# Batch normalisation of 64 tiles: from one DMA ring in phases of two to two DMA rings, with another placement of channels and parameters

## The chip, the cores and the metric

The kernel runs on one core of a Trainium2 chip. Its time is the device time of one execution in microseconds (us); where several runs are given, the median. One further execution was recorded by the hardware profiler, and all views below are of that one. The engines that matter here are SyncE (SP), which issues DMAs and does no arithmetic; VectorE (DVE); ScalarE (ACT), which computes and can issue DMAs too; GpSimd (POOL), which issues DMAs that its software describes; and the 16 DMA engines, which move the data between the main memory (HBM) and the on-chip memory (SBUF, 128 partitions).

## The reference

```python
# x: [32, 256, 128, 128] float32; the four parameters: [256] float32
def reference(x, gamma, beta, running_mean, running_var):
    eps = 1e-5
    mean = running_mean.reshape(1, -1, 1, 1)
    var = running_var.reshape(1, -1, 1, 1)
    gamma = gamma.reshape(1, -1, 1, 1)
    beta = beta.reshape(1, -1, 1, 1)
    return gamma * (x - mean) / np.sqrt(var + eps) + beta
```

Each of the 256 channels has one scale, gamma / sqrt(var + eps), and one shift, beta - mean x scale. Every element is read once, multiplied and added once, and written once: 536.87 MB in and as much out.

## The kernel before

The input is cut into 64 tiles, one for each image and each half of its channels. A tile has 128 channels on 128 partitions and 16384 floats (64 KB) in each: 8.39 MB. Channel p of the half lies on partition p (lines 38 and 39). Three buffers hold tiles (NBUF, line 11), 64 KB a partition each.

All big DMAs, loads (line 48) and stores (line 97), are issued by SP, so they lie in one ring and run in the order of issue. At first three loads are issued. Then the loop at line 100 goes through the tiles in pairs (K = 2): VectorE transforms two tiles in place (line 86, one instruction a tile), SP issues the two stores, and then two loads, of the tiles three further on, each into the buffer of a tile just stored. The framework sets the waits: a store waits for VectorE, a load for the store that frees its buffer. The ring so sees two stores, two loads, two stores, and so on.

The parameters come at the start. GpSimd issues four DMAs (line 56), each of which spreads 256 values over 128 partitions, two to a partition, element by element. ScalarE takes the square root (line 71) and VectorE works out scale and shift in lines 78 to 81. The first tile's transform needs both.

Of the kernel before, what the change touches and what calls it, by code (L numbers as in the profile page):

```python
# [1 line left out]

# [4 lines left out]


SINGLE_QUEUE = True  # L10
NBUF = 3


@with_exitstack
def kernel(
    ctx: ExitStack,
    tc: tile.TileContext,
    x: bass.AP,
    gamma: bass.AP,
    beta: bass.AP,  # L20
    running_mean: bass.AP,
    running_var: bass.AP,
    out: bass.AP,
):
    nc = tc.nc
    eps = 1e-5

    N, C, H, W = x.shape
    P = nc.NUM_PARTITIONS
    assert C % P == 0  # L30
    NCB = C // P
    HW = H * W
    NT = N * NCB

    params = ctx.enter_context(tc.tile_pool(name="params", bufs=1))
    data = ctx.enter_context(tc.tile_pool(name="data", bufs=NBUF))

    xr = x.rearrange("n (cb p) h w -> (n cb) p (h w)", p=P)
    outr = out.rearrange("n (cb p) h w -> (n cb) p (h w)", p=P)

    tiles = {}
    loads = {}

    def issue_load(i):
        if i >= NT:
            return
        t = data.tile([P, HW], mybir.dt.float32, tag="t")
        loads[i] = nc.sync.dma_start(out=t[:], in_=xr[i])  # L48
        tiles[i] = t

    for i in range(NBUF):
        issue_load(i)

    def load_param(ap_1d):
        t = params.tile([P, NCB], mybir.dt.float32, tag=ap_1d.tensor.name)
        nc.gpsimd.dma_start(out=t, in_=ap_1d.rearrange("(j p) -> p j", p=P))  # L56
        return t

    var_t = load_param(running_var)
    gamma_t = load_param(gamma)  # L60
    beta_t = load_param(beta)
    mean_t = load_param(running_mean)

    eps_t = params.tile([P, 1], mybir.dt.float32, tag="eps")
    nc.vector.memset(eps_t, eps)  # L65

    scale_t = params.tile([P, NCB], mybir.dt.float32, tag="scale")
    shift_t = params.tile([P, NCB], mybir.dt.float32, tag="shift")
    tmp_t = params.tile([P, NCB], mybir.dt.float32, tag="tmp")

    nc.scalar.activation(  # L71
        out=tmp_t[:],
        in_=var_t[:],
        func=mybir.ActivationFunctionType.Sqrt,
        bias=eps_t[:],
        scale=1.0,
    )
    nc.vector.reciprocal(out=tmp_t[:], in_=tmp_t[:])  # L78
    nc.vector.tensor_mul(out=scale_t[:], in0=gamma_t[:], in1=tmp_t[:])  # L79
    nc.vector.tensor_mul(out=tmp_t[:], in0=mean_t[:], in1=scale_t[:])  # L80
    nc.vector.tensor_sub(out=shift_t[:], in0=beta_t[:], in1=tmp_t[:])  # L81

    def compute(i):
        t = tiles[i]
        cb = i % NCB
        nc.vector.tensor_scalar(  # L86
            out=t[:],
            in0=t[:],
            scalar1=scale_t[:, cb : cb + 1],
            scalar2=shift_t[:, cb : cb + 1],  # L90
            op0=mybir.AluOpType.mult,
            op1=mybir.AluOpType.add,
        )

    def store(i):
        t = tiles.pop(i)
        (nc.sync if SINGLE_QUEUE else nc.scalar).dma_start(out=outr[i], in_=t[:])  # L97

    K = NBUF - 1
    for b in range((NT + K - 1) // K):  # L100
        idxs = [i for i in range(K * b, K * b + K) if i < NT]
        for i in idxs:
            compute(i)
        for i in idxs:
            store(i)
        for i in idxs:
            issue_load(i + NBUF)


# [1 line left out]
_INS = ['x', 'gamma', 'beta', 'running_mean', 'running_var']  # L111
_OUTS = [((32, 256, 128, 128), 'float32')]


# [23 lines left out]
```

## Time and profile before

| what | value |
|---|---|
| median of 8 runs | 2487.67 us (2486.35 to 2489.26) |
| the profiled execution's own time | 2486.76 us |
| its span, first to last instruction | 2484.7 us |
| moved by DMA, and mean rate over the span | 1073.77 MB, 432 GB/s |
| one VectorE transform of a tile | 8.81 us, 64 of them |
| load, median from issue to landing | 38.6 us |
| store, median from issue to landing | 49.8 us |
| parameter DMAs, issue to landing | 10.8, 15.4, 19.7 and 21.7 us |
| first transform starts | 25.72 us |

The page gives busy times for each engine; a DMA's time from issue to landing includes its place in the ring behind earlier ones. In the timeline a line has start, duration, engine, line of the kernel and operation; "SPq" is SP's queue, where merged issues ("x2") have the time from the first issue to the end of the last, waits between them included. What stands in brackets is the engine's idle time before, and what ended it. In the table of windows, each line has the stretch, its length, the busy time of VectorE, ScalarE and GpSimd with the number of instructions, TensorE's clock, the busy share of the 16 DMA engines, and the rate in GB/s.

### The profile page before, as it was taken

The numbers are of one execution on the slowest core, as the hardware profiler recorded it, in microseconds if no ns is written. First come the engines' busy times: TensorE is split into PE (matmuls) and PEld (weight loads), VectorE is DVE, ScalarE is ACT, GpSimd is POOL, SyncE is SP. The second block draws the span as 40 slices with busy tenths as digits, with TensorE's granted clock in tenths as the row PEclk, the third lists the DMA queues.
The fourth block names the chain that finished last, engine by engine and source line by source line (L and its number), as shares of the span: only waits on it lengthen the run. The fifth ranks groups of instructions, "written<-read, shape, count | busy, mean of one in ns | idle before, by whom it ended". The sixth has DMA issues, their size and how long they took to land.

```text
span 2484.7 us, 378 instructions
## 1 busy us (share of the span) xinstructions
DVE 564.7 (23%) x69; ACT 1.6 (0%) x2; POOL 3.2 (0%) x8
## 2 busy tenths in 40 slices
DVE  2122211222112221122211222122221212212121
ACT  0000000000000000000000000000000000000000
POOL 0000000000000000000000000000000000000000
DMA  9999999999999999999999999999999999999999
GB/s 405 439 436 425 437 434 428 438 434 435 430 435 436 427 436 437 433 431 439 433 429 438 437 433 430 438 432 435 435 434 436 430 438 432 436 434 434 436 430 397
DMA packets 18562, 1073.77 MB, mean 432 GB/s; under 512 B 2176, under 2 KB 2176, under 8 KB 2176
## 3 DMA queue, kind: packets, MB, share of 16 engines
q1 hardware_dynamic: 18432, 1073.75, 99.9%
q0 software_dynamic: 128, 0.00, 0.0%
q14 instruction: 2, 0.02, 0.0%
HBM read 536.88 MB, written 536.87 MB: 432 GB/s over the span
## 4 chain that ended last, share of the span: by engine, by line
DMA 51%; another core or an unknown queue 36%; DVE 11%; SPq 0%; issue 0%; POOL 0%; DVEq 0%; POOLq 0%; PEldq 0%
DMA t<-in_x_dram 48%; DVE t L86 11%; DMA out_dram<-t 2%; DMA t<-in_running_mean_dram 1%; SPq L97 0%; POOL t L56 0%; DVEq L86 0%; POOLq L133 0%; SPq L48 0%; DVE tmp_t L80 0%; DVE shift_t L81 0%; DVEq L80 0%; PEldq L133 0%
## 5 line engine op out<-in xcount | busy, mean ns | idle before, releaser
L86 DVE TENSOR_SCALAR t<-t,scale_t,shift_t 128x16384 f32<-128x16384 f32 x64 | 564.0, 8812 | 1864.4 <-DMA t<-in_x_dram 1864.4
L78 DVE RECIPROCAL tmp_t<-tmp_t 128x2 f32<-128x2 f32 x1 | 0.2, 165 | 12.9 <-ACT tmp_t L71 12.9
L80 DVE TENSOR_TENSOR tmp_t<-t,scale_t 128x2 f32<-128x2 f32 x1 | 0.2, 160 | 7.6 <-DMA t<-in_running_mean_dram 7.6
L71 ACT ACT_TABLE_LOAD x1 | 1.3, 1283 | 12.1 <-DMA t<-in_running_var_dram 12.1
L79 DVE TENSOR_TENSOR scale_t<-t,tmp_t 128x2 f32<-128x2 f32 x1 | 0.2, 161 | 3.7 <-DMA t<-in_gamma_dram 3.7
L56 POOL DMA_DIRECT2D t<-in_running_var_dram x1 | 0.8, 837 | 0.8 <-PEq L133 0.8
L56 POOL DMA_DIRECT2D t<-in_gamma_dram x1 | 0.7, 722 | 0.0
L56 POOL DMA_DIRECT2D t<-in_beta_dram x1 | 0.7, 720 | 0.0
L56 POOL DMA_DIRECT2D t<-in_running_mean_dram x1 | 0.7, 720 | 0.0
L71 ACT ACTIVATE tmp_t<-t,eps_t 128x2 f32<-128x2 f32 x1 | 0.3, 295 | 0.0
L65 DVE MEMSET eps_t<- 128x1 f32 x1 | 0.1, 59 | 0.8 <-PEq L122 0.8
L81 DVE TENSOR_TENSOR shift_t<-t,tmp_t 128x2 f32<-128x2 f32 x1 | 0.2, 160 | 0.0
L122 POOL MEMSET const-bfloat16-1.0<- 128x1 bf16 x1 | 0.1, 95 | 0.0
L122 POOL MEMSET const-float32-0.0<- 128x1 f32 x1 | 0.1, 93 | 0.2 <-issue 0.2
L122 POOL MEMSET const-uint8-127<- 128x1 uint8 x1 | 0.1, 93 | 0.0
L122 POOL MEMSET const-float32-1.0<- 128x1 f32 x1 | 0.1, 92 | 0.0
## 6 DMA issues: line engine op xcount, KB each, us to landing
t<-in_x_dram SPq DMA_DIRECT2D x64, 38.6
out_dram<-t SPq DMA_DIRECT2D x64, 49.8
t<-in_running_var_dram POOLq DMA_DIRECT2D x1, 1.0 KB, 10.8
t<-in_gamma_dram POOLq DMA_DIRECT2D x1, 1.0 KB, 15.4
t<-in_beta_dram POOLq DMA_DIRECT2D x1, 1.0 KB, 19.7
t<-in_running_mean_dram POOLq DMA_DIRECT2D x1, 1.0 KB, 21.7
```

The costliest lines, as they stand in the source:

```text
L56: nc.gpsimd.dma_start(out=t, in_=ap_1d.rearrange("(j p) -> p j", p=P))
L65: nc.vector.memset(eps_t, eps)
L71: nc.scalar.activation(out=tmp_t[:], in_=var_t[:], func=mybir.ActivationFunctionType.Sqrt, bias=eps_t[:], scale=1.0,)
L78: nc.vector.reciprocal(out=tmp_t[:], in_=tmp_t[:])
L79: nc.vector.tensor_mul(out=scale_t[:], in0=gamma_t[:], in1=tmp_t[:])
L80: nc.vector.tensor_mul(out=tmp_t[:], in0=mean_t[:], in1=scale_t[:])
L81: nc.vector.tensor_sub(out=shift_t[:], in0=beta_t[:], in1=tmp_t[:])
L86: nc.vector.tensor_scalar(out=t[:], in0=t[:], scalar1=scale_t[:, cb : cb + 1], scalar2=shift_t[:, cb : cb + 1], op0=mybir.AluOpType.mult, ...
L122: nc = _bacc.Bacc("TRN2", target_bir_lowering=False, num_devices=1)
```

## The change

- The kernel no longer leaves its waits to the framework: it has a semaphore for each buffer's loads and stores, one for VectorE's finished parts and a few for the start, and each instruction's wait is written out.
- Loads stay on SP; stores go to ACT's queue, each waiting for its tile's transform. There are no pairs any more: tile i's load waits for the store of tile i - 3, the transform for the load, the store for the transform.
- Channels are placed otherwise: channel 16k + e of a half lies on partition 8e + k, in loads and stores alike. The DRAM side of a DMA so has the form 16 x 8 x 16384.
- The parameters come as rows: SP loads each vector of 256 values as one row of 1 KB, copied to 16 partitions, between the left and the right half of load 0. VectorE puts each row into the order of the partitions, transposes it in 32 x 32 blocks, and copies four pieces of the result to the partitions' columns. Square root, scale and shift are worked out as before.
- Tile 0 is loaded and transformed in two halves. Of the last tile, VectorE transforms the first 9216 columns and ScalarE the other 7168.

```diff
-    xr = x.rearrange("n (cb p) h w -> (n cb) p (h w)", p=P)
-    outr = out.rearrange("n (cb p) h w -> (n cb) p (h w)", p=P)
+    xr = x.rearrange("n (cb k e) h w -> (n cb) e k (h w)", k=NK, e=NE)
+    outr = out.rearrange("n (cb k e) h w -> (n cb) e k (h w)", k=NK, e=NE)
...
-        t = params.tile([P, NCB], mybir.dt.float32, tag=ap_1d.tensor.name)
-        nc.gpsimd.dma_start(out=t, in_=ap_1d.rearrange("(j p) -> p j", p=P))
...
+        nc.sync.dma_start(out=bufs[0][:, left], in_=xr[0][:, :, left]).then_inc(early, 16)
+        zeroed = step(nc.vector.memset(rows[:], 0.0))
+        for r, ap in enumerate((running_var, gamma, beta, running_mean)):
+            inst = nc.sync.dma_start(out=rows[0:NE, r * C : (r + 1) * C], in_=ap.partition_broadcast(NE))
+            if r == 0:
+                inst._wait_ge(vec, zeroed)
+            inst.then_inc(fetched, 16)
+        nc.sync.dma_start(out=bufs[0][:, right], in_=xr[0][:, :, right]).then_inc(loaded[0], 16)
+        for i in range(1, NT):
+            s, turn = i % NBUF, i // NBUF
+            inst = nc.sync.dma_start(out=bufs[s][:], in_=xr[i]).then_inc(loaded[s], 16)
+            if turn:
+                inst._wait_ge(stored[s], 16 * turn)
...
+        step(
+            nc.vector.tensor_copy(
+                out=lined.rearrange("p (rc e k) -> p rc e k", e=NE, k=NK),
+                in_=rows.rearrange("p (rc k e) -> p rc e k", k=NK, e=NE),
+            ),
+            fetched,
+            16 * NPAR,
         )
...
+        step(nc.vector.transpose(out=turned[:], in_=lined[:]))
...
+        for q in range(NQ):
+            placed = step(nc.vector.tensor_copy(out=flat[q * B : (q + 1) * B], in_=blocks[:, :, q, 0]))
...
-        (nc.sync if SINGLE_QUEUE else nc.scalar).dma_start(out=outr[i], in_=t[:])
...
+            nc.scalar.dma_start(out=outr[i], in_=bufs[s][:])._wait_ge(done, after).then_inc(stored[s], 16)
...
-    K = NBUF - 1
-    for b in range((NT + K - 1) // K):
-        idxs = [i for i in range(K * b, K * b + K) if i < NT]
-        for i in idxs:
-            compute(i)
-        for i in idxs:
-            store(i)
-        for i in idxs:
-            issue_load(i + NBUF)
...
+        compute(0, left)._wait_ge(early, 16)
+        compute(0, right)._wait_ge(loaded[0], 16)
+        store(0, 2)
+        for i in range(1, last):
+            compute(i)._wait_ge(loaded[i % NBUF], 16 * (i // NBUF + 1))
+            store(i, i + 2)
...
+        compute(last, slice(0, VCOLS))._wait_ge(loaded[last % NBUF], 16 * turns)
+        t, cb = bufs[last % NBUF], last % NCB
+        nc.scalar.activation(
+            out=t[:, VCOLS:],
+            in_=t[:, VCOLS:],
+            func=mybir.ActivationFunctionType.Identity,
+            bias=shift_t[:, cb : cb + 1],
+            scale=scale_t[:, cb : cb + 1],
+        )._wait_ge(loaded[last % NBUF], 16 * turns).then_inc(done, 1)
+        store(last, last + 3)
```

## The prediction

> **What bounds the kernel now.** I read the page's busy times and DMA row first, then the queues, then the waits, then the timeline for the cadence, then windows of the DMA rate for the two ends.
>
> ```profile
> DVE 564.7 (23%) x69; ACT 1.6 (0%) x2; POOL 3.2 (0%) x8
> DMA  9999999999999999999999999999999999999999
> q1 hardware_dynamic: 18432, 1073.75, 99.9%
> q0 software_dynamic: 128, 0.00, 0.0%
> L86 DVE TENSOR_SCALAR t<-t,scale_t,shift_t 128x16384 f32<-128x16384 f32 x64 | 564.0, 8812 | 1864.4 <-DMA t<-in_x_dram 1864.4
> ```
>
> VectorE works a quarter of the span and waits for loads for the rest of it. The one hardware queue fills 99.9% of what 16 DMA engines have. So the kernel is 1073.75 MB pushed through a full pipe, and only two things can move it: the rate of the pipe, and the time in which part of it is empty.
>
> ```profile
> 83.10 19.92 SPq L48 DMA_DIRECT2D t<-in_x_dram  x2
> 103.07 28.08 SPq L97 DMA_DIRECT2D out_dram<-t  x2
> 121.96 8.81 DVE L86 TENSOR_SCALAR t<-t,scale_t,shift_t 128x16384 f32<-128x16384 f32 x1 [49.35 <-DMA t<-in_x_dram]
> 141.78 8.81 DVE L86 TENSOR_SCALAR t<-t,scale_t,shift_t 128x16384 f32<-128x16384 f32 x1 [11.01 <-DMA t<-in_x_dram]
> 161.10 19.70 SPq L48 DMA_DIRECT2D t<-in_x_dram  x2
> ...
> 2406.59 0.34 SPq L48 DMA_DIRECT2D t<-in_x_dram  x1
> 2407.03 47.45 SPq L97 DMA_DIRECT2D out_dram<-t  x2
> ```
>
> This is the cadence: a pair of loads is issued as a pair of stores lands, 78.0 us after the last pair (161.10 - 83.10). Such a period moves four tiles of 8.39 MB. The timeline has the same issue at 1092.57, so 13 early periods take (1092.57 - 83.10) / 13 = 77.65 us, and the 17 later ones (2406.59 - 1092.57) / 17 = 77.30 us, or 19.32 us for a tile and 434 GB/s. The late cadence is the pipe's own; the early periods are 13 x 0.35 = 4.6 us longer.
>
> ```profile
> 0.00:5.00 5.00, 0.06 (x1) 0.00 (x0) 3.19 (x8) 1.00 0.76 262
> 5.00:10.00 5.00, 0.00 (x0) 0.00 (x0) 0.00 (x0) 1.00 1.02 367
> 10.00:25.00 15.00, 0.33 (x2) 1.58 (x2) 0.00 (x0) 1.00 1.01 420
> 1213.00:1985.00 772.00, 175.26 (x21) 0.00 (x0) 0.00 (x0) 1.00 1.00 434
> 2448.00:2484.70 36.70, 6.11 (x1) 0.00 (x0) 0.00 (x0) 1.00 0.85 368
> ```
>
> The last two columns are DMA share and GB/s. The start runs below 434, and in the last 37 us the mean engine is busy only 85% of the time: 5.5 us each. The engines don't finish together, and the slowest ends the kernel.
>
> **The budget of the profiled span.** 128 tile transfers x 19.32 = 2473.5 us. The third load lands at 63.79 (its VectorE instruction starts then), where three tiles would take 58.0: start 5.8 us. Early periods: 4.6. After the last cadence point, 2406.59 + 4 x 19.32 = 2483.9: end 0.8. Sum 2484.7, the span. No more than about 11 us can be won while the rate stays: 0.45%.
>
> [...]
> **The change, part by part.**
> *Parameters.* Removed: four POOL DMAs of 4-byte elements (the 128 packets of q0), which land 10.8 to 21.7 us after issue. Added: four SP DMAs of 1 KB rows in 16 copies[...], queued between the two halves of load 0. The first load took 24.3 us to land (the least of the issue-to-landing times)[...]. A 1 KB row at a 16th of 434 GB/s is 0.04 us; with overhead I take 0.1, four for each engine 0.4, and as much for the split load's second completion. So between 0 and 3.0 us are won, and I take 3.0 - 0.8 = 2.2. SP waits for a memset of 32x1024 before the parameter DMAs[...]. Behind it wait the right half of load 0 and loads 1 and 2; the left half already queued covers 9.7 us, so nothing is lost[...].
> *Turning by VectorE.* A copy and a transpose of 32x1024, four small copies, the square root with its table load (1.28 + 0.29 in the trace), and four operations of 0.16 each. [...]Cost 0: loads 1 and 2 keep the pipe full to about 60 us, and the first store merely comes near 30 instead of 34.56. It would have to be 30 us late to be felt.
> *Two rings.* Stores move from SP behind the load issues to ACT behind VectorE's semaphore; loads on SP wait for their buffer's store only. With both rings always filled, each gets half the rate: load 38.6, VectorE 8.8, store 38.6[...]: 90 us for a buffer's round, and three buffers at 38.6 a tile give it 116. So 26 us of slack: the pipe does not run dry, and no new wait is exposed. Cost of alternation itself, not seen in the trace: between 0 and 1% of rate[...]; I take 0.
> *Dealt channels.* [...]By number of packets and bytes nothing changes. Whether the 4.6 us of the early periods and the 5.5 us of uneven ends are address collisions is unknown: between 0 and 9 us won[...], or a loss if the same pattern collides elsewhere. I take 4.2, a little less than half.
> *Shared last tile.* VectorE does 9216 of 16384 columns, 4.96 us by proportion of 8.81, ScalarE the rest. In the half-rate picture, when load 63 lands the store of tile 62 has some 13 us to go, so even 8.8 us was hidden: 0, and at most 3.9 us.
>
> Sum against the profiled run: 2484.7 - 2.2 - 4.2 = 2478.3 span. Around the span lay 2486.76 - 2484.7 = 2.1, giving 2480.4. That run was 0.9 below the median of 2487.67, so a median of 2481. Its own range is 2475 (all of start and early periods gone: 2487.67 - 3.0 - 9 is 2475.7) to 2482.7.
>
> **Rivals.** A measurement of this kernel can tell about 0.2%, 5.0 us, from no change; so faster is below 2482.7, slower above 2492.6.
> - *The forecast*, 2481, chance 0.42. For it: the pipe is full, its rate is the limit in both directions, and the losses lie where the change reaches.
> - *Nothing but the parameters*, 2487.67 - 2.2 = 2485.5, chance 0.20. The early periods and uneven ends come from the engines, not the addresses, and stay. For it: every period already runs within 1% of the limit.
> - *Alternating loads and stores on an engine costs rate*, chance 0.34. Place: every row while both rings are full, about 2400 us. Price: each 1% is 24 us, and from 0.27% on (6.5 us, or 6.5 ns on a row of 19.32 / 8 = 2.415 us) it eats the forecast's gain; beyond 0.47% the kernel is slower. At 1%: 2481 + 24 = 2505. For it: before, each phase of one direction lasts 38.6 us and an engine seldom turns[...]. Against: the late periods include two turns each, with engines out of step, and stay at 77.3.
> - [...], chance 0.04. [...]No trace shows who gets which partition. Here too belongs a form that spreads over fewer engines.
>
> **How the numbers follow.** Faster 0.42 is the forecast; same 0.20 is the second case; slower 0.38 the last two. Single time 2481. The range runs from 2475 to 2510: the low end is the forecast's, and the high end takes the alternation up to 1.2%; about 0.15 lies outside, mostly above.
>
> **What would show it.** The period of loads: under 38.65 us for each tile pair and flat from the start if the dealing helps; longer early if not; 39.0 and more all along if alternation costs. The first load landing near 22 to 23 us shows the parameters. A DMA share above 0.85 in the last 37 us shows evener ends. If the DMA share stays at 99% while GB/s drops below 432, the rows themselves are longer, and my zero for alternation is wrong; if the share falls, a buffer wait is, and my 26 us of slack.

## The result, and the profile after

| what | before | after |
|---|---|---|
| median | 2487.95 us (31 runs) | 3397.67 us (11 runs, 3333 to 3475) |
| ratio, after to before | | 1.350, 95% interval 1.347 to 1.354 |
| profiled execution, its span | 2486.76, 2484.7 us | 3417.79, 3416.0 us |
| mean DMA rate over the span | 432 GB/s | 314 GB/s |

The kernel became slower by 35%, where 2481 us was forecast. The ratio leaves the slower, disturbed executions out, so it lies a little below that of the two medians. These lines of the page after have the DMA share, the rate, the two rings (q1 is SP's, q10 ACT's) and VectorE:

```profile
DMA  9999999999999999999999999999999999999997
GB/s 236 300 318 323 316 305 327 316 316 314 304 305 311 314 320 318 318 323 302 342 309 311 337 320 338 333 327 315 332 325 310 325 307 328 318 313 326 344 317 214
q1 hardware_dynamic: 9488, 536.94, 59.5%
q10 hardware_dynamic: 9216, 536.88, 40.0%
L134 DVE TENSOR_SCALAR t<-t,scale_t,shift_t 128x16384 f32<-128x16384 f32 (+2 forms) x65 | 560.5, 8624 | 2771.3 <-DMA t<-in_x_dram 2771.1
```

The DMA engines are as busy as before, and VectorE works as long as before (560.5 us; 564.0 before). But the same bytes come through at 314 GB/s. So the engines do not stand idle for want of work: the transfers themselves take longer. Nearly equal bytes on the two rings (536.94 and 536.88 MB) take unequal shares of engine time: loads (q1) 59.5%, stores (q10) 40.0%. Where the loss begins can be read from windows of the changed kernel (stretch, length, VectorE, ScalarE, GpSimd, clock, DMA share, GB/s):

```profile
5.00:10.00 5.00, 0.00 (x0) 0.00 (x0) 0.00 (x0) 1.00 0.93 190
10.00:25.00 15.00, 0.00 (x0) 0.00 (x0) 0.00 (x0) 1.00 1.00 203
64.00:441.00 377.00, 61.69 (x7) 0.00 (x0) 0.00 (x0) 1.00 1.00 313
1213.00:1985.00 772.00, 132.19 (x15) 0.00 (x0) 0.00 (x0) 1.00 1.00 320
3300.00:3416.00 116.00, 13.89 (x2) 6.36 (x1) 0.00 (x0) 1.00 0.84 234
```

From 10 to 25 us there are only loads, since no store is issued before 49.4 us, and they already run at 203 GB/s, under half of 434. So alternating loads and stores can't be the first cause. When stores join, the rate rises, to 313 GB/s from 64 us on. A price for alternation would do the opposite.

### The profile page after: what moved, and what is told of

Read it like the earlier page. It is cut to its first block, busy times and chain, and to the rows that moved or that the text cites. A ratio compares the mean times of both kernels' runs of the same rounds, so it can differ in the third digit from the quotient of the medians.

```text
span 3416.0 us, 267 instructions
## 1 busy us (share of the span) xinstructions
DVE 565.1 (17%) x77; ACT 7.9 (0%) x3; POOL 0.2 (0%) x4
## 3 DMA queue, kind: packets, MB, share of 16 engines
q1 hardware_dynamic: 9488, 536.94, 59.5%
q10 hardware_dynamic: 9216, 536.88, 40.0%
HBM read 536.94 MB, written 536.87 MB: 314 GB/s over the span
## 4 chain that ended last, share of the span: by engine, by line
another core or an unknown queue 81%; DVE 16%; DMA 1%; ACT 0%; issue 0%; SPq 0%; ACTq 0%; DVEq 0%
DVE t L134 16%; DMA t<-in_x_dram 1%; ACT t L157 0%; SPq L91 0%; DVE rows L89 0%; ACTq L145 0%; DVE eps_t L102 0%; DVEq L193 0%; SPq L70 0%
## 5 line engine op out<-in xcount | busy, mean ns | idle before, releaser
L134 DVE TENSOR_SCALAR t<-t,scale_t,shift_t 128x16384 f32<-128x16384 f32 (+2 forms) x65 | 560.5, 8624 | 2771.3 <-DMA t<-in_x_dram 2771.1
L104 DVE COPY lined<-rows 32x1024 f32<-32x1024 f32 x1 | 1.0, 1024 | 23.6 <-DMA rows<-in_running_mean_dram 23.6
```

Source lines behind the costliest of these rows:

```text
L104: nc.vector.tensor_copy(out=lined.rearrange("p (rc e k) -> p rc e k", e=NE, k=NK), in_=rows.rearrange("p (rc k e) -> p rc e k", k=NK, e=NE),),
L134: return nc.vector.tensor_scalar(out=t[:, cols], in0=t[:, cols], scalar1=scale_t[:, cb : cb + 1], scalar2=shift_t[:, cb : cb + 1], op0=myb ...
```

## The experiments

Three explanations were open. "Dealing" is used here for placing channel 16k + e on partition 8e + k. Its loss could come from the partitions that the rows go to (the last of the forecast's rivals, with a chance of 0.04). It could come from the addresses in HBM. Or alternating rings could cost the time.

**Only the channels dealt, one ring.** The kernel before with

```diff
-    xr = x.rearrange("n (cb p) h w -> (n cb) p (h w)", p=P)
+    xr = x.rearrange("n (cb k e) h w -> (n cb) e k (h w)", k=8, e=16)
```

the same for the output, and the parameters placed alike.

> The kernel before, one ring, with only the channels dealt (16 x 8 on the DRAM side; the parameters dealt alike). Dealing is the cause[...]: the changed kernel's loads ran at 203 GB/s before any store, so a load takes about 40 us instead of 19.3; if stores do the same, 64 x 80 = 5150 us, and the second ring even won time; if only loads do, 64 x 60 = 3800. Alternating rings are the cause: 2488, as before. The DMA share stays at 0.99 in each case.

Measured: 4641.51 us, ratio 1.851 (1.848 to 1.855). This is its timeline, in which stores and loads still come in pairs:

```profile
2046.30 36.62 SPq L48 DMA_DIRECT2D t<-in_x_dram  x2
2082.97 49.29 SPq L99 DMA_DIRECT2D out_dram<-t  x2
2122.84 8.81 DVE L88 TENSOR_SCALAR t<-t,scale_t,shift_t 128x16384 f32<-128x16384 f32 x1 [99.96 <-DMA t<-in_x_dram]
2160.66 8.81 DVE L88 TENSOR_SCALAR t<-t,scale_t,shift_t 128x16384 f32<-128x16384 f32 x1 [29.02 <-DMA t<-in_x_dram]
2192.64 36.40 SPq L48 DMA_DIRECT2D t<-in_x_dram  x2
```

A period of four transfers is 146.3 us (2192.64 - 2046.30) instead of 77.3. The second load lands 37.8 us after the first (2160.66 - 2122.84). The second store lands about 36 us after the first: 36.62 us span the two load issues, the second of which waits for it. Both directions pay. So dealing alone does more harm than the whole change, and something else in the change took part of it back; the second ring is tried for this below.

**Two rings without dealing.** The changed kernel with channel p on partition p again.

> The changed kernel with channel p back on partition p; rings, parameter rows and the shared last tile stay. Dealing is the cause: near my forecast, 2481 (2475 to 2492). Alternating loads and stores on an engine is the cause or part of it: above 2500, up to 3400 if it is all.

Measured: 2497.97 us (2483.53 to 2514.86), ratio 1.0036 (1.0018 to 1.0053). The 35% are gone, and dealing alone had brought a loss, so dealing is the cause. What remains is a small loss instead of the small gain forecast; it is taken up below.

**Partitions or HBM addresses.** Two kernels that differ in one number, the first partition, tell the two apart, since everything in HBM is the same. Both copy x to the output in tiles of 64 channels, in a form of 16 x 4, and leave out scale and shift; in the second run BASE is 0. That partitions 0 to 63 would be slow and 32 to 95 fast was the author's assumption; no run had shown it. Each expectation has the case of the partitions first and that of the addresses second.

```diff
+    BASE, PT = 32, 64
...
+    xr = x.rearrange("n (cb k e) h w -> (n cb) e k (h w)", k=4, e=16)
...
+        nc.sync.dma_start(out=t[BASE : BASE + PT], in_=xr[i])
```

> A copy of x to the output through SBUF (scale and shift are left out), one ring, 128 tiles of 64 channels dealt 16 x 4 onto partitions 32 to 95. [...]full rate, 434 GB/s and about 2480 to 2500. HBM addresses are the cause: half rate like the change's loads, 4000 to 5200.

> The same copy on partitions 0 to 63, everything in HBM as in the run on 32 to 95. [...]half rate, 217 GB/s and about 4950. HBM addresses are the cause: the same time as on 32 to 95, whatever that is.

Measured: on 32 to 95, 2487.03 us, ratio 0.9999 (0.9991 to 1.0007); on 0 to 63, 4731.02 us, ratio 1.898 (1.890 to 1.906). The pages, first on 32 to 95:

```profile
DMA packets 20482, 1073.77 MB, mean 432 GB/s; under 512 B 4096, under 2 KB 4096, under 8 KB 4096
q1 hardware_dynamic: 20480, 1073.76, 99.9%
```

and on 0 to 63:

```profile
DMA packets 20482, 1073.77 MB, mean 228 GB/s; under 512 B 4096, under 2 KB 4096, under 8 KB 4096
q1 hardware_dynamic: 20480, 1073.76, 99.4%
```

The two runs have the same packets, the same bytes, the same access pattern in HBM and engines as busy (99.9% and 99.4%), but 228 GB/s on 0 to 63, little more than half the rate. So the choice of partitions decides here; by what means, no trace shows. HBM addresses fall as the cause, since rows dealt in the same way run at 432 GB/s on 32 to 95.

**The form or the neighbours.** Two more placements in the kernel before, one ring. The first keeps one outer dimension of 128 but spreads the rows (partition p has channel 2p or 2p + 1). The second has the 16 x 8 form, but its 16 groups begin 1 MB apart. The output and the parameters are placed alike.

```diff
+    xr = [x[i // 2].rearrange("(p cb) h w -> cb p (h w)", p=P)[i % 2] for i in range(NT)]
...
+    xr = [x[i // 2].rearrange("(e cb k) h w -> cb e k (h w)", e=16, k=8)[i % 2] for i in range(NT)]
```

> The kernel before, but partition p has channel 2p or 2p + 1: another placement with rows 128 KB apart, while the DRAM side keeps one outer dimension of 128. If what matters is the 16 x 8 form (who gets which partitions), 2488 as before. If the spacing of rows in HBM matters, another time, up to the change's.

> The kernel before with a 16 x 8 form, but no neighbouring channels side by side: group e takes eight successive channels, the groups are 1 MB apart. If the form decides[...], about 4640 as with dealt channels. If the neighbouring rows decide, 2488.

Measured: 2487.61 us, ratio 0.9994 (0.9986 to 1.0002), for the spread rows; 4647.19 us, ratio 1.869 (1.866 to 1.873), for the 16 x 8 form. The page of the 16 x 8 form:

```profile
GB/s 208 227 250 247 231 233 230 240 239 228 234 229 237 236 231 227 225 235 239 230 227 224 237 236 230 229 225 235 242 238 225 223 235 239 232 225 225 234 238 190
q1 hardware_dynamic: 18432, 1073.75, 99.0%
```

So in these runs it doesn't matter which channels go where; the form of the DRAM side does: a ratio of 0.9994 with one dimension of 128, and of 1.851 and 1.869 with 16 x 8. With 16 x 4 a split form alone cost nothing on 32 to 95 (0.9999) and nearly doubled the time on 0 to 63 (1.898). That the 16 x 8 form too is slow by its partitions is inferred from these four one-ring runs: the trace shows no partition of a packet. A 16 x 8 form with its groups laid on the partitions in another way was not run; it would have shown whether anything else in the form costs time.

**Why the change was not as slow as one ring.** These are the copy on partitions 0 to 63 with stores on the second ring, and the same on 32 to 95. Loads and stores here are also issued tile by tile instead of in pairs, so the two edits are not told apart. The first expectation has two cases: each direction is free of the other, or one limit holds for both together.

```diff
-        nc.sync.dma_start(out=outr[i], in_=t[BASE : BASE + PT])
+        nc.scalar.dma_start(out=outr[i], in_=t[BASE : BASE + PT])
...
-    K = NBUF - 1
+    K = 1
```

> The copy on partitions 0 to 63 (scale and shift left out), with stores on ACT's ring and one tile at a time. [...]each direction keeps its half rate while the other runs, so towards 2500[...]. [...]4730 as on one ring, and the way from 4642 to 3398 in the change is something else.

> The same on partitions 32 to 95: dealt channels, two rings[...]. If dealing helps[...], below the natural two-ring run's 2498 and below 2480. If it does nothing, 2485 to 2515 with the spread of that run, its engines out of step at the end.

Measured: on 0 to 63, 3567.27 us, ratio 1.437 (1.432 to 1.442); on 32 to 95, 2487.45 us (2483.68 to 2507.17), ratio 1.0004 (0.9990 to 1.0018). On 0 to 63 a second ring shortens 4731 to 3567, by a factor of 1.33; in the dealt kernel it shortens 4642 to 3398, by 1.37. The page on 0 to 63 also has the unequal rings of the changed kernel:

```profile
DMA packets 20484, 1073.79 MB, mean 304 GB/s; under 512 B 4096, under 2 KB 4096, under 8 KB 4096
q1 hardware_dynamic: 10240, 536.88, 61.3%
q10 hardware_dynamic: 10240, 536.88, 38.5%
```

On 32 to 95 the two rings have 50.2% and 49.8%. The like factors and the like shares speak for the same effect in both kernels: transfers that are slow by their placement gain when loads and stores have a ring each and go tile by tile. Neither case was met in full: the limit isn't one for both directions together, which would be 4730, but at 3567 instead of about 2500 the directions are far from free of each other. Why the gain stops at 304 GB/s was not settled. On 32 to 95, dealing with two rings is level with the kernel before in the median, though 7 of its 14 executions (2483.68 to 2484.61) were below the fastest of the kernel before on the same chip (2485.91).

**The start alone.** This is the run without dealing, with stores back on SP in pairs and the last tile all on VectorE.

```diff
-            nc.scalar.dma_start(out=outr[i], in_=bufs[s][:])._wait_ge(done, after).then_inc(stored[s], 16)
+            nc.sync.dma_start(out=outr[i], in_=bufs[s][:])._wait_ge(done, after).then_inc(stored[s], 16)
...
+        K = NBUF - 1
+        for b in range(0, NT, K):
+            for i in range(b, b + K):
+                store(i, i + 2)
+            for i in range(b + NBUF, min(b + NBUF + K, NT)):
+                load(i)
```

> The run with channel p on partition p, but stores back on SP in pairs between the loads, as before; the last tile all on VectorE. What is new against the kernel before is the start alone (parameter rows, split first load). The second ring's drift of the engines is what cost the natural two-ring run its 10 us: here the end is even again, DMA share 0.85 or more in the last 37 us, and the time is 2487.7 - 2.2 = 2485.5 (2483 to 2487.5). The start is what cost them: about 2498.

Measured: 2487.74 us, ratio 0.9999 (0.9991 to 1.0007). Its timeline at both ends:

```profile
81.68 19.98 SPq L98 DMA_DIRECT2D t<-in_x_dram  x2
...
2408.03 0.34 SPq L98 DMA_DIRECT2D t<-in_x_dram  x1
```

The first pair of loads is issued 1.4 us earlier than before (81.68; 83.10 before), and the last load 1.4 us later (2408.03; 2406.59 before). In this profile the start won something: the whole first tile was in by 23.6 us, close to the 22 to 23 forecast. Longer periods in between, 2.9 us in all, took it back. The expected 2.2 us are not there in the median. The end is as even as before, a DMA share of 0.87 from 2448 to 2486 us, as expected; before, it was 0.85 from 2448 us to the end of the span. Since this kernel is level with the one before, the loss of the run without dealing belongs to what the two do not share: the second ring, and with it the order tile by tile and the shared last tile.

**Where the second ring's 10 us lie.** These are windows of the two-ring run without dealing. Its profiled execution took 2506.63 us, 20 us more than the one before:

```profile
64.00:441.00 377.00, 79.55 (x10) 0.00 (x0) 0.00 (x0) 1.00 1.00 434
441.00:1213.00 772.00, 176.25 (x20) 0.00 (x0) 0.00 (x0) 1.00 1.00 433
1213.00:1985.00 772.00, 176.26 (x20) 0.00 (x0) 0.00 (x0) 1.00 1.00 430
1985.00:2440.00 455.00, 99.64 (x12) 0.00 (x0) 0.00 (x0) 1.00 1.00 431
2440.00:2505.00 65.00, 11.19 (x2) 6.36 (x1) 0.00 (x0) 1.00 0.78 336
```

At first both rings together run at 434, so for these 377 us the second ring costs nothing. Later the rate falls to 430 and 431 with the engines still full: compared with 434, that is 7.1 and 3.1 us (estimates from the lines: 772 x 4 / 434 and 455 x 3 / 434). At the end the mean engine is idle for 22% of 65 us, 14 us, against 6 us in the last 65 us of the kernel before. So about half of the 20 us lies in the rate and half at the end. A closer view of this end, and two windows of the kernel before (its last 65 us, and its last transform):

```profile
2460.00:2470.00 10.00, 0.00 (x0) 0.00 (x0) 0.00 (x0) 1.00 0.80 347
2470.00:2475.90 5.90, 0.00 (x0) 0.00 (x0) 0.00 (x0) 1.00 0.36 156
2475.90:2482.30 6.40, 5.08 (x1) 6.36 (x1) 0.00 (x0) 1.00 0.17 72
```

```profile
2419.70:2484.70 65.00, 8.81 (x1) 0.00 (x0) 0.00 (x0) 1.00 0.91 395
2445.00:2454.00 9.00, 8.70 (x1) 0.00 (x0) 0.00 (x0) 1.00 0.94 408
```

With two rings the last load lands at 2475.93, when most engines have run out of work. Then they wait for the last tile's transform: a share of 0.17 over 6.4 us is 5.3 us idle. In the kernel before, the share was 0.94 during the last transform, because the store of the tile before still ran. To see whether all engines only wait for the slowest one's last load, the last tile was cut into four column pieces:

```diff
+        for j, cols in enumerate(pieces):
+            compute(last, cols)._wait_ge(piece[j], 16)
+            nc.scalar.dma_start(out=outr[last][:, cols], in_=bufs[s][:, cols])._wait_ge(done, last + 2 + j).then_inc(stored[s], 16)
```

> The natural two-ring run with the last tile loaded, transformed and stored in four column pieces. If its 10 us over the kernel before are the wait of all engines for the slowest one's last load, then the last store hides under that load except for a quarter: 8 us less, 2490, and a DMA share above 0.78 in the last 65 us. If the loss is longer rows in the middle, it stays near 2498.

> The natural two-ring kernel once more beside the one with four pieces, for its spread and a second profile: 2484 to 2515, and a profile that falls low should have a busier end, one that falls high an emptier one, with the middle alike.

Measured: in four pieces 2503.46 us, ratio 1.0053 (1.0034 to 1.0072); again as it was 2497.88 us, ratio 1.0044 (1.0027 to 1.0062). The pieces gained nothing, and the DMA share in the last 65 us is about 0.80 (an estimate from the 0.84 measured from 2430 to 2498 us), where the whole tile had 0.78. In their timeline the last piece lands no earlier than the whole tile did in the first two-ring profile (2475.93), but later:

```profile
2445.30 2.41 DVE L142 TENSOR_SCALAR t<-t,scale_t,shift_t 128x4096 f32<-128x4096 f32 x1 [3.26 <-DMA t<-in_x_dram]
2467.12 2.41 DVE L142 TENSOR_SCALAR t<-t,scale_t,shift_t 128x4096 f32<-128x4096 f32 x1 [19.40 <-DMA t<-in_x_dram]
2478.65 2.41 DVE L142 TENSOR_SCALAR t<-t,scale_t,shift_t 128x4096 f32<-128x4096 f32 x1 [9.12 <-DMA t<-in_x_dram]
2488.36 2.41 DVE L142 TENSOR_SCALAR t<-t,scale_t,shift_t 128x4096 f32<-128x4096 f32 x1 [7.29 <-DMA t<-in_x_dram]
```

The first piece lands in good time and the fourth 43 us later, for a quarter of a tile each. This fits an engine that is behind with its own share, so that cutting the work doesn't help it; but the stores of the first pieces also run between the later loads, and the run does not tell the two apart. The second profile did not sort the runs as expected either: it took 2500.14 us where the first took 2506.63, and its end was no busier (a share of 0.77 in its last 68 us, about 0.79 in those of the first, an estimate from the 0.78 of its last 65). The loss is not the same in every execution either: 5 of the 22 of the first two-ring run were below the fastest of the kernel before on the same chip (2485.51), and 13 above its slowest (2492.73). That engines get out of step fits the ends; what makes one fall behind, and why the rate falls, stays open.

No version was found that beats the kernel before: the best two, one ring with the new start and spread rows, are level with it within 0.15%.

## Why the prediction was wrong

- *What bounds the kernel:* right. The pipe was full before and is full after. The sign named for a wrong step also came, a DMA share of 0.99 with a rate below 432 (314), "the rows themselves are longer". But I had tied it to the alternation; here it came with the placement, from the first loads on.
- *The failed step: dealt channels.* "By number of packets and bytes nothing changes" is true, and the price, between 0 and 9 us won with 4.2 taken, was worked out from HBM addresses alone. What failed is the step from there to an unchanged rate. The runs show the form and the partitions in its place: the 16 x 8 form takes 1.85 to 1.87 times the time on one ring and 1.35 on two, and the choice of partitions alone makes the same copy take 1.90 or 1.00 times as long. No gain from dealing was seen either: the copy on 32 to 95 gives 0.9999, though it also has smaller tiles and no parameters. The rival that had the loss in the placement on the partitions got a chance of 0.04, because no trace shows who gets which partition. That the trace is silent was no evidence for a small chance, and the range took none of it in.
- *Two rings, alternation at 0:* mis-sized by 9 to 11 us, 1.0036 and 1.0044 in the runs without dealing. The forecast's bound, 0 to 1% of rate, held it, but in the profile about half of the loss lay at the end, which that bound was not about; the last tile's share of it follows below. The profiled run reached 429 GB/s over its span, 432 before. The buffers' slack held as well, 26 us by the author's estimate (load 38.6, VectorE 8.8 and store 38.6 us leave 30 of 116): the DMA share is 1.00 in the middle of that run.
- *Parameters, 2.2 us won:* an estimate of the author's; measured as 0 with the new start on one ring, between a gain of 2.2 us and a loss of 1.7 (0.9991 and 1.0007 of 2488). In the profile the first pair came 1.4 us earlier and the last load later, so the term had the right sign at its place, but the budget's other terms did not stay put.
- *Turning by VectorE:* right to be free: without dealing, its chain ended at 18.0 us and the first store came at 28.1 us, near the 30 forecast.
- *Shared last tile, 0:* wrong in the run without dealing. The forecast hid the transform under the store of tile 62; there that store was all but done (a DMA share of 0.36 from 2470 us until the last load landed), and the transform's 6.4 us left the mean engine 5.3 us idle. The split itself shortened them from 8.8 us. A finer cut won nothing in the median, so what it would be worth to hide them stays open.

## What to carry to other kernels

In a kernel that is bound by DMA, look at the form of each access pattern and at the partitions it goes to, not only at its bytes: here two placements that move the same bytes in rows of the same length differ by a factor of 1.87, and only one has a single outer dimension; one copy on two choices of partitions differs by 1.90. Test a new form alone, with a plain copy, before building around it; the first 25 us of a profile, where only loads run, were enough to see this loss. And where the profile cannot show a resource, give the case that it is lost a chance that matches that ignorance.

## What the runs showed that was not expected

- 64 partitions can carry the full rate: with the 16 x 4 form, 32 to 95 moved 432 GB/s, 0 to 63 only 228.
- Issuing a DMA of the 16 x 8 form takes its queue longer: 0.536 us for a load in the changed kernel, 0.328 with one dimension of 128.
- A ring of its own for stores, with loads and stores tile by tile, gives back part of the loss on 0 to 63: 304 GB/s instead of 228.
- With two rings and one dimension of 128, single runs spread by 31 us (2483.53 to 2514.86), while the kernel before on the same chip spread by 7 us (2485.51 to 2492.73).
